# The first loads on two queues and x transposed one piece ahead, in fixed order: one encoder layer in exact-split fp32, one Trainium2 core

## The chip, the cores and the metric

The kernel runs on one core of a Trainium2 chip. The metric is the device time of one execution in microseconds (us). The engines of the core are named as the profile names them: PE is TensorE (PEld its weight loads), DVE is VectorE, ACT is ScalarE, POOL is GpSimd, SP is SyncE, whose queue issues DMAs.

## The reference

One layer on 256 tokens with 2048 channels: a gated bidirectional recurrence (HGRN2) as mixer, then a gated MLP with a depthwise convolution, each between RMS norms and with a residual.

```python
h = rmsnorm(x, norm_pre_mix)                   # (256, 2048)
u = h @ w_in                                   # (2048, 10240): q | f_fwd | f_bwd | i | g
m = gated(bidirectional_recurrence(u)) @ w_out
x = x + rmsnorm(m, norm_post_mix)
h = rmsnorm(x, norm_pre_ffn)
up = dwconv3(h @ ffn_w_in, ffn_w_conv)         # (2048, 11264)
x = x + rmsnorm((silu(gate) * val) @ ffn_w_out, norm_post_ffn)
```

This document is about the beginning alone: the first two products, which are columns of `q` and of `f_fwd`.

## The kernel before, in words

**Weights.** Every matrix is cut into chunks of 512 columns, and a chunk into *parts* of 256 rows (two k-blocks of 128). `load` fetches four k-blocks, one megabyte, into a tile `raw` (three buffers), which makes two parts. `prep` splits a part into a high and a low half: ScalarE rounds it to `whi` (L129, CAST), VectorE subtracts to give `wlo` (L130). There are four buffers of each. The first `raw` is loaded in four pieces of 256 KB and the second in two of 512 KB; from the third on a load is one DMA of a megabyte. So the first `raw` holds parts 0 and 1, the second parts 2 and 3, the third (the first whole megabyte) parts 4 and 5.

**x.** `xs` holds x as it is in memory, tokens on partitions, loaded in pieces of 256, 256, 512, 512 and 512 columns by `load_x`. `split_x(k2)` turns one *piece* of 256 columns: four PE transposes into a PSUM tile `tp` (L287), two ScalarE instructions that scale it into the high half of `xx` (L291), and two of VectorE that make the low half (L295). The scale comes from `prm`, a table of parameters. Part s of a product needs piece s of `xx`.

**The product.** `gemm_t` runs over eight parts; in each, for four column blocks n and two k-blocks, one matmul with `whi` (L204, 512 columns wide) and one with `wlo` (L206, 256 wide), sixteen a part. The first product takes a `pre` that is called at the head of part s and turns a piece ahead. Each later product looks three parts ahead with `prep`, the first one none (`LOOK if ci else 1`).

**Order.** A scheduler puts the instructions of each engine into an order at build time, by priorities that follow the program's order and by its own estimate of times; on the chip each engine then runs its list in that order. `tc.keep_in_program_order` fixes the place of an instruction against the others so marked. Semaphores are set by the framework: a DMA that uses one of eight DMA semaphores again first waits for the DMA that had it before.

The matmuls of `warm` (L266) run while the first data are on their way.

Of the kernel before, what the change touches and what calls it, by code (L numbers as in the profile page):

```python
# [18 lines left out]
P = 128  # L19
T = 256  # L20
D = 2048
KT = D // P
# [19 lines left out]
C_CW = C_LB + 2 * NH  # L42
# [4 lines left out]
def encoder_layer(  # L47
# [12 lines left out]
    nc = tc.nc  # L60
# [17 lines left out]
    prm = const.tile([P, C_END], F32, name="prm")  # L78
    ident = const.tile([P, P], F32, name="ident")
# [22 lines left out]
    def step():  # L102
        if soon or later:
            (soon or later).popleft()()

    def load(pieces=1):
        ci, s = subs[at["load"]]
        wd, c, _ = chunks[ci]
        raw = wraw.tile([P, 4, 512], F32, name="raw", tag="raw")
        src = wd[c, s // 2].rearrange("p (k n) -> p k n", n=512)  # L110
        w = 4 // pieces
        raws[ci, s // 2] = raw
        at["load"] += 2
        for i in range(pieces):
            nc.sync.dma_start(raw[:, w * i : w * i + w], src[:, w * i : w * i + w])
            yield

    def prep(upto):
        while at["prep"] < min(upto, len(subs)):
            i = at["prep"]  # L120
            if at["load"] <= i:
                list(load())
            ci, s = subs[i]
            src = raws[ci, s // 2][:, 2 * (s % 2) : 2 * (s % 2) + 2, :]
            pl, sfx = (extra[0], str(s)) if ci == C_UP - 1 and s >= 2 * chunks[ci][2] - 4 else (wspl, "")
            hi = pl.tile([P, 2, 512], F32R, name="whi", tag="whi" + sfx)
            lo = pl.tile([P, 2, 512], F32R, name="wlo", tag="wlo" + sfx)
            for j in [slice(0, 1), slice(1, 2)] if i == 0 else [slice(0, 2)]:
                S.copy(hi[:, j], src[:, j])  # L129
                V.tensor_tensor(lo[:, j], src[:, j], hi[:, j].bitcast(F32), op=ALU.subtract)  # L130
            parts[ci, s] = (hi, lo)
            at["prep"] += 1
# [3 lines left out]
    def flush():  # L136
        while soon or later:
            step()
# [46 lines left out]
    def gemm_t(xx, need=None, pre=None):  # L185


        ci = at["chunk"]
        at["chunk"] += 1
        nsub = 2 * chunks[ci][2]  # L190
        base = subs.index((ci, 0))
        ps = [ps_g.tile([P, 2, T], F32, name="pg", tag="pg") for _ in range(4)]
        for s in range(nsub):
            if s == need:
                flush()
            if pre:
                pre(s)
            prep(base + s + (LOOK if ci else 1))
            hi, lo = parts[ci, s]
            for n in range(4):  # L200
                cs = slice(n * P, (n + 1) * P)
                for j in range(2):
                    k = 2 * s + j
                    nc.tensor.matmul(ps[n], hi[:, j, cs], xx[:, k], start=(k == 0), stop=False)  # L204
                    last = k == 2 * nsub - 1
                    nc.tensor.matmul(ps[n][:, 0, :], lo[:, j, cs], xx[:, k, 0, :], start=False, stop=last)  # L206
            step()
        return ps
# [29 lines left out]
    xx = acts.tile([P, KT, 2, T], F32R, name="xx", tag="xx")  # L238
# [3 lines left out]
    xs = spool.tile([P, 2, D], F32, name="xs")  # L242

    def load_x(a, b):
        nc.sync.dma_start(xs[:, :, a:b], x_v[:, :, a:b])

    nc.sync.dma_start(prm[:, :C_CW], par[:, :C_CW])
    load_x(0, 256)
    first = load(4)
    next(first), next(first)  # L250
    load_x(256, 512)
    list(first)
    load_x(512, 1024)
    list(load(2))
    load_x(1024, 1536)
    load_x(1536, 2048)
# [25 lines left out]
    def split_x(k2):  # L282
        tp = ps_t.tile([P, 2, T], F32, name="tp", tag="tp")
        for j in range(2):
            k = 2 * k2 + j
            for m in range(2):
                nc.tensor.transpose(tp[:, j, m * P : (m + 1) * P], xs[:, m, k * P : (k + 1) * P], ident)  # L287
        for j in range(2):
            k = 2 * k2 + j
            w1 = prm[:, C_PRE + k : C_PRE + k + 1]  # L290
            S.activation(xx[:, k, 0, :], tp[:, j, :], AF.Copy, scale=w1)  # L291
        for j in range(2):
            k = 2 * k2 + j
            w1 = prm[:, C_PRE + k : C_PRE + k + 1]
            V.scalar_tensor_tensor(  # L295
                xx[:, k, 1, :], tp[:, j, :], w1, xx[:, k, 0, :].bitcast(F32), op0=ALU.mult, op1=ALU.subtract
            )
# [3 lines left out]
    def square_x(q):  # L301
        for m in range(2):
            jk = spool.tile([P, 512], F32, name="jk", tag="jk", bufs=2)
            i = 4 * m + q
            c = slice(q * 512, (q + 1) * 512)
            tc.keep_in_program_order(S.activation(jk, xs[:, m, c], AF.Square, accum_out=ss1[:, i : i + 1]))

    def mean_x():
# [3 lines left out]
        soon.extend([nop, lambda: spread(rs1, r1)])  # L312

    split_x(0)
    split_x(1)
    ps0 = gemm_t(xx, pre=lambda s: split_x(s + 2) if 2 * s + 4 < KT else None)
    soon.extend([lambda q=q: square_x(q) for q in range(4)] + [mean_x])
    ps1 = gemm_t(xx)
    load_rest()
    sstack.close()  # L320
# [26 lines left out]
    def do_q(g):  # L347
        ps = gemm_t(xx) if g else ps0
        qT = hp.tile([P, HG, T], F32, name="qT", tag="qT")
        each_token(ps, qT, r1)  # L350
        sg = nat.tile([P, HG, T], F32, name="qn", tag="qn")
        S.activation(sg, qT, AF.Sigmoid)
        V.tensor_tensor(qT, qT, sg, op=ALU.mult)
        st["q", g] = qT
# [174 lines left out]
    ps0 = gemm(oo, need=6)  # L529
# [84 lines left out]
    ps0 = gemm(hh, "head")  # L614
# [58 lines left out]
    ps0 = gemm(gg, need=20)  # L673
# [74 lines left out]
```

## Time and profile before

| | us |
|---|---|
| median of 3 runs | 1379.18 (1378.73 to 1380.75) |
| the profiled execution | 1379.42 |
| its span, first to last instruction | 1377.6 |
| TensorE busy in it | 1364.7 |
| end of the first product, q | 35.5 |
| end of the second product, f | 58.5 |

Span and rows are of one profiled execution. A row of the timeline has start and duration in us, engine, line, operation, output and inputs, and in brackets the idle time ahead of it with what ended it. A row of waits has who waited for whom, the total, the number of times and the longest. A row of DMA issues has the count, the size of one and the time from issue to landing. A row of stretches has busy time and count of PE, PEld, DVE, ACT and POOL, then TensorE's granted clock, the share of the DMA engines and GB/s.

### The profile page before, as it was taken

The page shows a single profiled execution, that of the slowest core. Times are in us where ns is not written, and L with a number is a line of the kernel's source. Part 1 is how long each engine was busy: PE and PEld are TensorE (multiplying, and loading weights), DVE is VectorE, ACT ScalarE, POOL GpSimd, SP SyncE. Part 2 cuts the span into 40 slices and gives each one's busy share as a digit, 9 for nine tenths or more (in the row PEclk, how much of TensorE's full clock was granted, in tenths as well). Part 3 has the DMA queues.
Part 4 walks back from the last instruction along what each step waited for, and adds up shares of the span by engine and source line. Part 5 has one row for each costly group of instructions (what it writes and reads, how often), then busy time and mean ns, then how long its engine had stood idle before and what let it go on. Part 6 is the DMA issues. An engine that isn't in the chain of part 4 may idle for free.

```text
span 1377.6 us, 18400 instructions
## 1 busy us (share of the span) xinstructions
PE 1364.7 (99%) x7362; PEld 1176.7 (85%) x7362; DVE 934.6 (68%) x1188; ACT 694.6 (50%) x971; POOL 13.5 (1%) x21
## 2 busy tenths in 40 slices
PE   8999999999999999999999999999999999999997
PEld 7888988898898888888888888888888888888886
DVE  6587668866886876567768676777677775445444
ACT  5644455454554544456656455555555554434442
POOL 0000000000000000000000000000000000000000
PEclk9999999999999999999999999999999999999999
DMA  7554355435534444673555545555555556555552
GB/s 286 180 187 149 125 181 184 153 123 183 184 134 168 166 144 153 245 245 109 197 183 184 193 176 210 183 186 182 188 186 192 194 190 214 191 204 185 189 207 93
DMA packets 36998, 248.93 MB, mean 181 GB/s; under 512 B 4144, under 2 KB 4912, under 8 KB 7472
## 3 DMA queue, kind: packets, MB, share of 16 engines
q1 hardware_dynamic: 36912, 247.75, 51.0%
q8 instruction: 58, 0.95, 0.3%
q14 instruction: 28, 0.23, 0.0%
HBM read 245.63 MB, written 2.10 MB: 180 GB/s over the span
## 4 chain that ended last, share of the span: by engine, by line
PE 97%; DVE 1%; issue 1%; ACT 0%; DMA 0%; SPq 0%; DVEq 0%; POOLq 0%; POOL 0%
PE pg L204 35%; PE pg L206 18%; PE pg L178 13%; PE pg L177 13%; PE pg L174 13%; PE sc L432 4%; PE sc L489 1%; PE sc L457 1%; PE sc L488 1%; PE sc L412 1%; DMA raw<-in_w_in 0%; PE tp L230 0%; PE tp L584 0%; PE tp L287 0%; DVE fw L685 0%
## 5 line engine op out<-in xcount | busy, mean ns | idle before, releaser
L130 DVE TENSOR_TENSOR wlo<-raw,whi 128x1024 fp32r<-128x1024 f32 (+1 forms) x457 | 555.2, 1221 | 381.6 <-ACT whi L129 374.8
L129 ACT CAST whi<-raw 128x1024 fp32r<-128x1024 f32 (+1 forms) x457 | 478.6, 1049 | 499.9 <-PE pg L204 259.3
L204 PE MATMUL pg<-hh,whi 128*128 128x512 f32 x1344 | 467.3, 397 | 0.0
L206 PE MATMUL pg<-hh,wlo 128*128 128x256 f32 x1344 | 366.1, 280 | 0.0
L204 PEld LDWEIGHTS pg<-hh,whi 128*128 128x128 f32 x1344 | 249.5, 188 | 56.2
L204 PE MATMUL pg<-xx,whi 128*128 128x512 f32 x768 | 270.0, 398 | 0.0
L206 PEld LDWEIGHTS pg<-hh,wlo 128*128 128x128 f32 x1344 | 253.4, 189 | 4.7
L206 PE MATMUL pg<-xx,wlo 128*128 128x256 f32 x768 | 211.0, 283 | 0.6 <-DVE wlo L130 0.6
L204 PEld LDWEIGHTS pg<-xx,whi 128*128 128x128 f32 x768 | 143.4, 188 | 30.7 <-DVE xx L295 0.4
L206 PEld LDWEIGHTS pg<-xx,wlo 128*128 128x128 f32 x768 | 145.4, 189 | 3.5 <-DVE wlo L130 1.1
L174 PE MATMUL pg<-whi,gg 128*128 128x512 f32 x352 | 137.0, 389 | 0.0
L178 PE MATMUL pg<-whi,gg 128*128 128x512 f32 x352 | 136.9, 389 | 0.0
L177 PE MATMUL pg<-wlo,gg 128*128 128x512 f32 x352 | 136.9, 389 | 0.0
L177 PE MATMUL pg<-wlo,xx 128*128 128x512 f32 x256 | 101.0, 394 | 0.0
L174 PE MATMUL pg<-whi,xx 128*128 128x512 f32 x256 | 100.2, 391 | 0.0
L178 PE MATMUL pg<-whi,xx 128*128 128x512 f32 x256 | 100.0, 391 | 0.0
L174 PEld LDWEIGHTS pg<-whi,gg 128*128 128x128 f32 x352 | 66.1, 188 | 13.9
L177 PEld LDWEIGHTS pg<-wlo,gg 128*128 128x128 f32 x352 | 66.1, 188 | 13.7
L178 PEld LDWEIGHTS pg<-whi,gg 128*128 128x128 f32 x352 | 66.1, 188 | 13.7
L432 PEld LDWEIGHTS sc<-qs,kc 128*128 128x128 f32 x448 | 57.7, 192 | 1.7
L432 PE MATMUL sc<-qs,kc 128*128 128x128 f32 x448 | 58.5, 285 | 0.0
L639 ACT ACTIVATE acc<-un,prm 128x256 f32<-128x256 f32 x84 | 38.2, 503 | 38.9 <-DVE un L345 38.8
(128 smaller groups left out, 1174.9 us busy)
## 6 DMA issues: line engine op xcount, KB each, us to landing
raw<-in_w_up SPq DMA_DIRECT2D x88, 1024.0 KB, 4.9
raw<-in_w_in SPq DMA_DIRECT2D x78, 1024.0 KB, 4.9
raw<-in_w_dn SPq DMA_DIRECT2D x44, 1024.0 KB, 4.9
raw<-in_w_o SPq DMA_DIRECT2D x16, 1024.0 KB, 4.9
x<-in_x SPq DMA_DIRECT2D x1, 2048.0 KB, 7.9
wp<-in_post SPq DMA_DIRECT2D x2, 1024.0 KB, 5.7
out<-fw SPq DMA_DIRECT2D x8, 256.0 KB, 2.6
xs<-in_x SPq DMA_DIRECT2D x3, 512.0 KB, 8.8
```

The lines of the kernel that those rows point to most:

```text
L129: S.copy(hi[:, j], src[:, j])
L130: V.tensor_tensor(lo[:, j], src[:, j], hi[:, j].bitcast(F32), op=ALU.subtract)
L174: mm = nc.tensor.matmul(ps[m], a, hi[:, j, :], start=(k == 0), stop=False)
L177: nc.tensor.matmul(ps[m], a, lo[:, j, :], start=False, stop=False)
L178: nc.tensor.matmul(ps[m], b, hi[:, j, :], start=False, stop=(k == 2 * nsub - 1))
L204: nc.tensor.matmul(ps[n], hi[:, j, cs], xx[:, k], start=(k == 0), stop=False)
L206: nc.tensor.matmul(ps[n][:, 0, :], lo[:, j, cs], xx[:, k, 0, :], start=False, stop=last)
L412: nc.tensor.matmul(sc[:, j, :], kc[0][:, h, sl], q[:, h, sl], start=True, stop=True)
L432: nc.tensor.matmul(sc[:, j, :], kc[0][:, h, sl], r, start=True, stop=True)
L457: nc.tensor.matmul(sc[:, h, :], ks[:, d, h, s0 : s0 + P], qs[:, 1 - d, h, t0 : t0 + P], start=True, stop=True)
L488: nc.tensor.matmul(o[:, h, :], Sd[:, 2 * h + b, :], v[:, b, cs], start=True, stop=False)
L639: S.activation(a, z, AF.Copy, scale=cw[1])
```

## The change

Two things. The four DMAs of the first `raw`, and the small one of `prm` between them, are issued from ScalarE's queue, and the pieces of x go first on SyncE's. And `split_x` is called for the piece of the next part alone, between the second and third of the four column blocks of a part (before: two pieces ahead of the loop, and piece s+2 at the head of part s); the transposes, and of each pair of k-blocks the first matmul with `whi`, are kept in program order. All lines behind move by two or three: L287, L291, L295 become L290, L295, L299, and L206 becomes L208.

```diff
-    def load(pieces=1):
+    def load(pieces=1, queue=nc.sync):
...
         for i in range(pieces):
-            nc.sync.dma_start(raw[:, w * i : w * i + w], src[:, w * i : w * i + w])
+            queue.dma_start(raw[:, w * i : w * i + w], src[:, w * i : w * i + w])
             yield
...
         for s in range(nsub):
             if s == need:
                 flush()
-            if pre:
-                pre(s)
             prep(base + s + (LOOK if ci else 1))
             hi, lo = parts[ci, s]
             for n in range(4):
+                if pre and n == 2:
+                    pre(s)
                 cs = slice(n * P, (n + 1) * P)
                 for j in range(2):
                     k = 2 * s + j
-                    nc.tensor.matmul(ps[n], hi[:, j, cs], xx[:, k], start=(k == 0), stop=False)
+                    mm = nc.tensor.matmul(ps[n], hi[:, j, cs], xx[:, k], start=(k == 0), stop=False)
+                    if pre and j == 0:
+                        tc.keep_in_program_order(mm)
...
-    nc.sync.dma_start(prm[:, :C_CW], par[:, :C_CW])
     load_x(0, 256)
-    first = load(4)
+    first = load(4, nc.scalar)
     next(first), next(first)
+    nc.scalar.dma_start(prm[:, :C_CW], par[:, :C_CW])
     load_x(256, 512)
     list(first)
...
             for m in range(2):
-                nc.tensor.transpose(tp[:, j, m * P : (m + 1) * P], xs[:, m, k * P : (k + 1) * P], ident)
+                tc.keep_in_program_order(
+                    nc.tensor.transpose(tp[:, j, m * P : (m + 1) * P], xs[:, m, k * P : (k + 1) * P], ident)
+                )
...
     split_x(0)
-    split_x(1)
-    ps0 = gemm_t(xx, pre=lambda s: split_x(s + 2) if 2 * s + 4 < KT else None)
+    ps0 = gemm_t(xx, pre=lambda s: split_x(s + 1) if 2 * s + 2 < KT else None)
```

What the scheduler makes of it is shown in rows of the built programs, with the semaphores that an instruction waits for. The numbers at names count tiles.

SyncE's queue at the start, before (`raw_87` is the first `raw`, `raw_94` the second, `raw_287` the first whole megabyte):

```order
L247 DMA prm_76<-in_par 128x65
L245 DMA xs_84<-in_x 128x2x256
L115 DMA raw_87<-in_w_in 128x512 x2
L245 DMA xs_84<-in_x 128x2x256
L115 DMA raw_87<-in_w_in 128x512 x2
L245 DMA xs_84<-in_x 128x2x512
L115 DMA raw_94<-in_w_in 128x1024 [waits DMAHW0_49]
L115 DMA raw_94<-in_w_in 128x1024 [waits DMAHW1_49]
L245 DMA xs_84<-in_x 128x2x512 [waits DMAHW2_49]
L245 DMA xs_84<-in_x 128x2x512 [waits DMAHW3_49]
L115 DMA raw_287<-in_w_in 128x2048 [waits DMAHW4_49]
```

Now, SyncE's queue (`raw_94` is still the second, `raw_269` the first whole megabyte):

```order
L247 DMA xs_84<-in_x 128x2x256 x2
L247 DMA xs_84<-in_x 128x2x512
L115 DMA raw_94<-in_w_in 128x1024
L115 DMA raw_94<-in_w_in 128x1024 [waits DMAHW0_49]
L247 DMA xs_84<-in_x 128x2x512 [waits DMAHW2_49]
L247 DMA xs_84<-in_x 128x2x512 [waits DMAHW3_49]
L115 DMA raw_269<-in_w_in 128x2048 [waits DMAHW4_49]
```

Five issues have left it. They stand at the head of ScalarE's list now, ahead of its table load and the first casts; the last of them waits for the first piece of x (DMAHW1):

```order
L115 DMA raw_86<-in_w_in 128x512 x2
L252 DMA prm_76<-in_par 128x65
L115 DMA raw_86<-in_w_in 128x512
L115 DMA raw_86<-in_w_in 128x512 [waits DMAHW1_49]
L129 ACT_TABLE_LOAD
L129 CAST whi_151<-raw_86 128x512 [waits DMAHW0_49]
L129 CAST whi_151<-raw_86 128x512 [waits DMAHW3_49]
```

ScalarE further on, before: the casts for parts 1 to 4 (`whi_200`, `229`, `258`, `289`) and the scalings of pieces 1 to 4 (`tp_147`, `160`, `191`, `220`):

```order
L291 ACTIVATE xx_80<-tp_147,prm_76 128x256 [waits PE_49]
L291 ACTIVATE xx_80<-tp_147,prm_76 128x256
L129 CAST whi_200<-raw_87 128x1024 [waits DMAHW6_49,DMAHW5_49]
L129 CAST whi_229<-raw_94 128x1024 [waits DMAHW0_49]
L291 ACTIVATE xx_80<-tp_160,prm_76 128x256 [waits PE_49]
L291 ACTIVATE xx_80<-tp_160,prm_76 128x256
L129 CAST whi_258<-raw_94 128x1024 [waits DMAHW1_49]
L291 ACTIVATE xx_80<-tp_191,prm_76 128x256 [waits PE_49]
L291 ACTIVATE xx_80<-tp_191,prm_76 128x256
L291 ACTIVATE xx_80<-tp_220,prm_76 128x256 [waits PE_49]
L291 ACTIVATE xx_80<-tp_220,prm_76 128x256
L129 CAST whi_289<-raw_287 128x1024 [waits DMAHW4_49,DVE_49]
```

Now: the casts for parts 1 to 5 are `whi_182`, `211`, `240`, `271`, `300`, the scalings of pieces 1 and 2 `tp_165` and `tp_194`:

```order
L129 CAST whi_182<-raw_86 128x1024 [waits DMAHW7_49,DMAHW1_49]
L129 CAST whi_211<-raw_94 128x1024 [waits DMAHW6_49]
L129 CAST whi_240<-raw_94 128x1024 [waits DMAHW0_49]
L295 ACTIVATE xx_80<-tp_165,prm_76 128x256 [waits PE_49]
L295 ACTIVATE xx_80<-tp_165,prm_76 128x256
L129 CAST whi_271<-raw_269 128x1024 [waits DMAHW4_49,PE_49,Activation_49]
L295 ACTIVATE xx_80<-tp_194,prm_76 128x256 [waits PE_49]
L295 ACTIVATE xx_80<-tp_194,prm_76 128x256
L129 CAST whi_300<-raw_269 128x1024 [waits DVE_49,PE_49]
```

The scaling of piece 1 has moved behind the casts for parts 1 to 3, that of piece 2 behind the cast for part 4; VectorE's list has its subtractions and low halves in the same new order.

TensorE at the seam of parts 0 and 1, now: the transposes of piece 1 in the middle of part 0, and behind its other half the first matmul of part 1, which waits for VectorE.

```order
L290 MATMUL tp<-ident,xs 128x128 [waits DMAHW2_49,PE_49]
L290 MATMUL tp<-ident,xs 128x128 x3
L204 MATMUL pg<-xx,whi 128x512
L208 MATMUL pg<-xx,wlo 128x256
L204 MATMUL pg<-xx,whi 128x512
L208 MATMUL pg<-xx,wlo 128x256
L204 MATMUL pg<-xx,whi 128x512
L208 MATMUL pg<-xx,wlo 128x256
L204 MATMUL pg<-xx,whi 128x512
L208 MATMUL pg<-xx,wlo 128x256
L204 MATMUL pg<-xx,whi 128x512 [waits DVE_49]
```

Before, two pieces were turned ahead of part 0 (eight transposes in a row) and the others stood one or two parts ahead of their own. From the second product on the lists of all engines are as before but for small exchanges (the load of the masks and one of weights, two squares of x and one cast).

## The prediction

> **What bounds the kernel now.** I read the page's busy times first, then TensorE's waits at the start, the timeline of TensorE over the first 60 us, the stretches with clock and DMA share, and last ScalarE's, VectorE's and SyncE's rows there.
>
> ```profile
> span 1377.6 us, 18400 instructions
> PE 1364.7 (99%) x7362; PEld 1176.7 (85%) x7362; DVE 934.6 (68%) x1188; ACT 694.6 (50%) x971; POOL 13.5 (1%) x21
> ```
> ```profile
> PE tp L287 <- DMA xs<-in_x: 2.8, 1, 2.8
> PE tp L266 <- POOL ident masks.py:199: 1.4, 1, 1.4
> PE pg L206 <- DVE wlo L130: 0.6, 1, 0.6
> ```
> TensorE is idle for 12.9 us of the span, and these are all its waits in the first 100 us. What a change at the start gains or loses is therefore what it does to the time at which TensorE has done its first two products, q and f. Each has eight parts (L204 and L206, sixteen matmuls a part).
>
> ```profile
> 4.99 0.60 PE L287 MATMUL tp<-ident,xs 128*128 128x128 f32 x4
> 8.38 1.08 PE L287 MATMUL tp<-ident,xs 128*128 128x128 f32 x4 [2.78 <-DMA xs<-in_x]
> 9.51 0.79 PE L204 MATMUL pg<-xx,whi 128*128 128x512 f32 x1
> ...
> 16.98 0.39 PE L204 MATMUL pg<-xx,whi 128*128 128x512 f32 x1
> ...
> 18.36 0.60 PE L287 MATMUL tp<-ident,xs 128*128 128x128 f32 x4
> 18.72 0.47 PE L204 MATMUL pg<-xx,whi 128*128 128x512 f32 x1
> ...
> 20.19 0.39 PE L204 MATMUL pg<-xx,whi 128*128 128x512 f32 x1
> ...
> 35.52 0.40 PE L204 MATMUL pg<-xx,whi 128*128 128x512 f32 x1
> ...
> 58.52 0.39 PE L204 MATMUL pg<-xx,whi 128*128 128x512 f32 x1
> ```
> Counting matmuls, part 0 starts at 9.51, part 2 at 16.98, part 3 at 20.19; the product q ends at 35.52 and f at 58.52. A part without transposes lasts (58.52 - 35.52)/8 = 2.87; a part with four transposes in its middle lasts 20.19 - 16.98 = 3.21, of which 1.83 lie from the first transpose (18.36) to the next part.
>
> ```profile
> 4.71:8.12 3.41, 0.88 (x8) 0.64 (x6) 0.69 (x1) 1.16 (x3) 0.00 (x0) 1.00 0.93 280
> 8.12:11.54 3.42, 3.12 (x10) 2.46 (x11) 2.68 (x6) 2.59 (x6) 0.00 (x0) 0.50 0.97 356
> 11.54:14.95 3.41, 3.41 (x23) 2.98 (x22) 2.22 (x2) 1.14 (x2) 0.00 (x0) 1.00 1.07 419
> 1.00:2.00 1.00, 0.64 (x3) 0.64 (x4) 0.00 (x0) 1.00 (x1) 0.29 (x1) 1.00 0.14 25
> 2.30:4.00 1.70, 1.70 (x10) 1.70 (x9) 1.07 (x5) 0.23 (x1) 0.00 (x0) 1.00 0.84 287
> 4.00:6.00 2.00, 1.59 (x11) 1.35 (x9) 0.51 (x4) 0.62 (x1) 0.00 (x0) 1.00 0.71 194
> 14.00:15.00 1.00, 1.00 (x10) 0.91 (x9) 0.76 (x1) 0.13 (x1) 0.00 (x0) 1.00 1.14 444
> 14.00:19.00 5.00, 5.00 (x35) 4.55 (x34) 3.65 (x6) 2.52 (x5) 0.00 (x0) 1.00 1.04 417
> ```
> The last three columns are clock, DMA share and GB/s. After a stretch with TensorE idle for 2.78 us the clock is 0.50 for 3.41 us. The DMA engines are full (share about 1) from 6 us on, and only partly used before.
>
> **The loads.** The same bytes are loaded as before.
>
> ```profile
> 0.74 0.39 SPq L247 DMA_DIRECT2D prm<-in_par  x1
> 1.18 0.42 SPq L245 DMA_DIRECT2D xs<-in_x  x1
> 8.26 0.34 SPq L115 DMA_DIRECT2D raw<-in_w_in  x1
> raw<-in_w_in SPq DMA_DIRECT2D x1, 1024.0 KB, 10.7
> xs<-in_x SPq DMA_DIRECT2D x1, 256.0 KB, 2.6
> 0.73 1.28 ACT L275 ACT_TABLE_LOAD   x1 [0.73 <-PEq L738]
> ```
> The load issued at 8.26 is the first whole megabyte of weights, for parts 4 and 5; it lands at 8.26 + 10.7 = 18.9. Ahead of it in both kernels stand all of x and two megabytes of weights, with it 5.28 MB. Five issues leave SyncE's queue for ScalarE's, so the first piece of x is issued at 0.74 in place of 1.18: 0.44 earlier. How long an issue takes on ScalarE no row shows; SyncE's take 0.39 to 0.47, so five take 0 to 2.3. I take 0.45 each; it hides, because the fifth waits anyway for the first piece of x. Two queues at once may also fill the engines' unused share, 1.70 x 0.16 + 2.00 x 0.29 = 0.85 us. So that megabyte lands between 18.9 - 0.44 = 18.5 and 17.6; I take the middle, 18.1. The far lower end is 5.28 MB at 417 GB/s from 1.7 on (an estimate of the first bytes at a start of 0.74, by the 25 GB/s of the second us), 14.4; the far upper end is no head start, 18.9.
>
> The Trainium skill (DMA: Bandwidth & Descriptors, "Issuing engines are not separate DMA queues") says that all issuers share the same 16 engines, and that issuing from several saves only the sequencer's issue time. By that rule the landing is 18.5 and the sum below 0.4 larger; the share of 1.04 from 14 to 19 agrees, while the 0.71 from 4 to 6 leaves room for more.
>
> **The first part.** ScalarE now issues four loads, waits for the first piece of x (1.18 + 2.6 = 3.8 before; now 0.74 + 2.6 and the same bytes of weights beside it, 0.26 MB at 194 to 444 GB/s, so 4.0 to 4.6), issues the fifth, then loads its table (1.28), casts two half pieces, and scales x. That gives 0.45 + 1.28 + 0.62 + 0.62 + 0.84, and 0.04 + 0.44 + 0.10 through VectorE to TensorE, 4.4 after the landing: part 0 starts at 8.4 to 9.0, 0.5 to 1.1 earlier than 9.51. It gains nothing: even with the clock at 0.50 throughout a window (1.7 lost) part 0 and its transposes end by 9.0 + 3.2 + 1.7 = 13.9, and what follows starts later.
>
> **The stall.** Program order decides here.
>
> ```profile
> 12.45 1.05 ACT L129 CAST whi<-raw 128x1024 fp32r<-128x1024 f32 x1 [1.18 <-DMA raw<-in_w_in]
> 14.87 0.84 ACT L291 ACTIVATE xx<-tp,prm 128x256 fp32r<-128x256 f32 x2 [1.36 <-PE tp L287]
> 19.00 0.84 ACT L291 ACTIVATE xx<-tp,prm 128x256 fp32r<-128x256 f32 x2 [1.62 <-PE tp L287]
> 16.68 1.23 DVE L130 TENSOR_TENSOR wlo<-raw,whi 128x1024 fp32r<-128x1024 f32 x1
> 19.88 0.88 DVE L295 SCALAR_TENSOR_TENSOR xx<-tp,prm,xx 128x256 fp32r<-128x256 f32 x2 [1.19 <-ACT xx L291]
> 5.25 0.62 ACT L129 CAST whi<-raw 128x512 fp32r<-128x512 f32 x1 [2.05 <-DMA raw<-in_w_in]
> ```
> At 12.45 a cast holds ScalarE for its weights' landing, with all behind it. Before, the scalings of x pieces 3 and 4 stand ahead of the cast for part 4. Now the scaling of piece 1 stands behind the casts of parts 1, 2 and 3, and that of piece 2 behind the cast of part 4; on VectorE likewise. So part 1 waits for the weights of part 3, and part 2 for the megabyte that only part 4 needs.
>
> Part 2: landing 18.1, cast 1.05, VectorE's subtraction 1.23 (ScalarE's scaling of 0.84 lies beside it), scaling on VectorE 0.44 for the first half, three hand-overs of 0.03 and one of 0.10: 2.9, so 21.0 in place of 16.98. Part 1 is earlier by two half megabytes of x and the megabyte, 2.1 MB at 417 GB/s = 5.0; it starts at 16.0, lasts 3.21 and ends at 19.2, so TensorE stands idle 2 to 4 us ahead of part 1 and 1.8 ahead of part 2.
>
> Then parts 2 to 4. From the first transpose to the next part TensorE has 1.83 of work; piece s+1 needs 0.64 (18.36 to 19.00) + 0.84 + 0.04 + 0.44 + 0.10 = 2.06. So each part waits 0.23 where nothing fills it: ahead of parts 3, 4, 5, together 0.7. Ahead of parts 6 and 7 half a part of f stands in between. That wait has no row before; its ends are 0 and, with a cast still running, 1.05 each; the chain above is nearest.
>
> From part 2 to the end of f: 3 x (3.21 + 0.23) + 2 x 3.21 + 2.87 + 23.0 = 42.6. So f ends at 21.0 + 42.6 = 63.6 in place of 58.52, **5.1 us later**. After that the order on every engine is as before but for one load of masks that changes place with one of weights; weights there arrive well ahead, I cost it at nothing, and if they came late the price is a wait like the 0.6 in the table of waits. TensorE is full for the rest, so the 5.1 stays. The profiled execution took 1379.42, 1.8 more than its span and 0.24 more than the median; 1379.42 + 5.1 = 1384.5, against the median 1384.3, which I forecast (likeliest case alone 1382.8 to 1385.4).
>
> **Rivals.** In short, the sum is (landing of that megabyte) - 13.0.
> - *The clock falls again.* The idle 1.8 to 2 us may leave TensorE at 0.50 in part 2; a window of 3.41 at half clock costs up to 1.7. In part 1 it is hidden by the wait for the megabyte. For it: 2.78 idle in one window sufficed. Against: 1.8 leaves the window half busy, and the next row with a busy 3.12 of 3.42 let it rise. Time 1384.3 + 1.7 = 1386.0. 22 in 100. The Trainium skill (TensorE: Matmul & The Clock Gate, "HAM oscillation") warns only of idle gaps above about 3.4 us; by that there is no fall, but the trace's gap of 2.78 differs, so I keep the chance.
> - *Two queues hurry the data, and the change is not slower.* If 5.28 MB land by 13.0 the loss is nil, and by 15.8 it is under 0.2%. At 444 GB/s, the best single us, from 1.7 on they land at 13.6: 1379.2 + 0.6 = 1379.8. Against: from 6 us on the engines' share is full already, and the slower rate up to then would have to double. 12 in 100.
> - *ScalarE isn't held at all* (casts find their weights there): then the start's 0.5 to 1.1, the 0.6 wait and the 1.0 or so lost at half clock could be saved, less 0.7 at the parts' seams: about 1377.5. The cast row with its 1.18 wait speaks against it. 3 in 100.
>
> **How the numbers follow.** The stall as summed 63, with the clock's fall 22, data hurried 12, not held 3. 0.2% is 2.8 us, about what a measurement of this kernel can tell from no change. Slower by more: 63 + 22, less a few where data come by 15.8, plus a few of the third: 0.85. Same 0.12, faster 0.03. The range reaches from a landing at 15.5 (1379.2 + 2.5 = 1381.7) to the clock's case with a landing at 18.9 (1379.2 + 5.9 + 1.7 = 1386.8).
>
> **What would show it.** In the changed profile: ScalarE's cast with a wait of about 2 us or more for the third megabyte, the scaling row behind it; TensorE waiting for VectorE's scaling 2 to 4 us ahead of part 1 and 2 ahead of part 2, then 0.2 each; part 2 near 21, the end of f near 63.6; first matmul of part 0 under 9.1. Wrong, if that megabyte lands under 16, if TensorE's waits sum to under 2 us after part 0, or if a new wait stands beyond 65 us.

## The result and the profile after

The changed kernel takes **1386.93 us** (median of 6 runs, 1385.88 to 1387.66) against 1379.5 for the kernel before on the same chip (6 runs, 1378.73 to 1380.75): ratio **1.0052, 95% interval 1.0041 to 1.0062**. It is slower, as forecast, and by more than forecast: 1386.93 lies 2.6 above the 1384.3 predicted and, in us, 0.1 above the upper end of the range. As a ratio it lies inside: 1.0052, where that end, 1386.8, is 1.0055 of 1379.18, since the kernel before took 0.3 more here than in its first runs. The profiled executions took 1386.11 and 1379.42, 6.7 apart.

The page's first lines of the changed kernel: the span has grown by 6.7 us, TensorE's busy time by 2.2.

```profile
span 1384.3 us, 18405 instructions
PE 1366.9 (99%) x7362; PEld 1177.4 (85%) x7362; DVE 934.3 (67%) x1188; ACT 694.8 (50%) x971; POOL 14.5 (1%) x21
```

TensorE's waits in its first 100 us (who waited for whom, us in total, times, longest), and with them one row of its weight loads, which is needed for the seams:

```profile
PE pg L204 <- DVE xx L299: 7.0, 2, 4.4
...
PEld pg L204 <- DVE xx L299: 9.2, 6, 4.8
...
```

Two waits for VectorE's scaling of x have taken the place of the one wait of 2.8 for x itself; the two other rows of TensorE's matmuls (1.4 and 0.6) are as before. Where they stand is told by TensorE's timeline (rows at which the wait or a part begins; counting matmuls, parts 0, 1, 2 and 3 start at 10.67, 18.10, 21.75 and 25.41, q ends at 42.19 and f at 65.13):

```profile
5.25 1.06 PE L290 MATMUL tp<-ident,xs 128*128 128x128 f32 x4
10.67 0.79 PE L204 MATMUL pg<-xx,whi 128*128 128x512 f32 x1 [4.36 <-DVE xx L299]
...
13.40 0.66 PE L290 MATMUL tp<-ident,xs 128*128 128x128 f32 x4
...
18.10 0.50 PE L204 MATMUL pg<-xx,whi 128*128 128x512 f32 x1 [2.65 <-DVE xx L299]
...
21.20 0.40 PE L204 MATMUL pg<-xx,whi 128*128 128x512 f32 x1
...
21.75 0.50 PE L204 MATMUL pg<-xx,whi 128*128 128x512 f32 x1
...
22.23 0.47 PE L204 MATMUL pg<-xx,whi 128*128 128x512 f32 x1
...
22.65 0.40 PE L204 MATMUL pg<-xx,whi 128*128 128x512 f32 x1
...
...
25.41 0.50 PE L204 MATMUL pg<-xx,whi 128*128 128x512 f32 x1
...
65.13 0.39 PE L204 MATMUL pg<-xx,whi 128*128 128x512 f32 x1
```

The end of f is 65.13 - 58.52 = 6.61 later, the span 6.7: nearly everything is lost in the first product, and 0.1 behind f. Part 0 is 1.2 later than before, part 1 4.8, part 2 4.8, part 3 5.2.

Why part 1 waits is read on the two engines ahead of it. ScalarE's timeline of the changed kernel, then VectorE's:

```profile
2.25 2.71 ACTq L115 DMA_DIRECT2D raw<-in_w_in  x2
4.98 1.28 ACT L129 ACT_TABLE_LOAD   x1 [4.98 <-DMA xs<-in_x]
...
9.27 0.84 ACT L295 ACTIVATE xx<-tp,prm 128x256 fp32r<-128x256 f32 x2 [0.93 <-DMA prm<-in_par]
...
13.08 2.94 ACT L129 CAST whi<-raw 128x1024 fp32r<-128x1024 f32 x3 [2.73 <-DMA raw<-in_w_in]
15.92 0.83 ACT L295 ACTIVATE xx<-tp,prm 128x256 fp32r<-128x256 f32 x2
18.57 1.05 ACT L129 CAST whi<-raw 128x1024 fp32r<-128x1024 f32 x1 [1.82 <-DMA raw<-in_w_in]
20.34 0.84 ACT L295 ACTIVATE xx<-tp,prm 128x256 fp32r<-128x256 f32 x2 [0.72 <-PE tp L290]
```
```profile
14.15 3.50 DVE L130 TENSOR_TENSOR wlo<-raw,whi 128x1024 fp32r<-128x1024 f32 x3 [1.99 <-ACT whi L129]
17.57 0.87 DVE L299 SCALAR_TENSOR_TENSOR xx<-tp,prm,xx 128x256 fp32r<-128x256 f32 x2
...
21.21 0.88 DVE L299 SCALAR_TENSOR_TENSOR xx<-tp,prm,xx 128x256 fp32r<-128x256 f32 x2 [0.33 <-ACT xx L295]
```

The transposes of piece 1 were done at 14.06. But ScalarE stood from 10.35 to 13.08 at the cast for part 1, whose weights had not landed, and then did the casts for parts 1, 2 and 3 in a row; VectorE did their three subtractions, 3.50 us, and only at 17.57 the low half that part 1 needs. Two of the three casts were for parts that TensorE reached at 21.75 and 25.41.

The DMA issues of the first 14 us (who, how many, size, median us from issue to landing), where `prm`, the table that every scaling needs, took 7.4 us in place of 1.8:

```profile
raw<-in_w_in SPq DMA_DIRECT2D x1, 1024.0 KB, 8.9
...
prm<-in_par ACTq DMA_DIRECT2D x1, 32.5 KB, 7.4
```

The whole megabyte was issued at 9.53 and landed at 18.47. Stretches of the changed kernel (busy PE, PEld, DVE, ACT, POOL, then clock, DMA share and GB/s):

```profile
2.00:4.00 2.00, 2.00 (x12) 2.00 (x11) 0.00 (x0) 0.00 (x0) 0.00 (x0) 1.00 0.89 265
4.00:6.00 2.00, 2.00 (x11) 1.91 (x9) 0.00 (x0) 1.02 (x1) 0.00 (x0) 1.00 0.93 197
6.70:10.10 3.40, 0.00 (x0) 0.00 (x0) 1.58 (x4) 1.65 (x4) 0.00 (x0) 1.00 1.04 395
10.12:13.53 3.41, 2.86 (x9) 2.47 (x10) 1.89 (x7) 0.68 (x2) 0.00 (x0) 0.50 1.03 399
13.53:16.94 3.41, 1.92 (x13) 1.47 (x11) 2.79 (x3) 3.22 (x5) 0.00 (x0) 1.00 1.07 411
```

### The profile page after: what moved, and what is told of

Read it like the earlier page. It is cut to its first block, busy times and chain, and to the rows that moved or that the text cites. A ratio compares the mean times of both kernels' runs of the same rounds, so it can differ in the third digit from the quotient of the medians.

```text
span 1384.3 us, 18405 instructions
## 1 busy us (share of the span) xinstructions
PE 1366.9 (99%) x7362; PEld 1177.4 (85%) x7362; DVE 934.3 (67%) x1188; ACT 694.8 (50%) x971; POOL 14.5 (1%) x21
## 4 chain that ended last, share of the span: by engine, by line
PE 97%; DMA 1%; DVE 1%; issue 1%; ACT 0%; DVEq 0%; POOLq 0%; POOL 0%
PE pg L204 35%; PE pg L208 18%; PE pg L177 12%; PE pg L174 12%; PE pg L178 12%; PE sc L435 4%; DMA raw<-in_w_in 1%; PE sc L492 1%; PE sc L460 1%; PE sc L491 1%; PE sc L415 1%; PE tp L232 0%; DMA xs<-in_x 0%; PE tp L587 0%; DVE wlo L130 0%
## 5 line engine op out<-in xcount | busy, mean ns | idle before, releaser
L208 PE MATMUL pg<-hh,wlo 128*128 128x256 f32 x1344 | 366.1, 280 | 0.0
L208 PEld LDWEIGHTS pg<-hh,wlo 128*128 128x128 f32 x1344 | 253.4, 189 | 4.7
L208 PE MATMUL pg<-xx,wlo 128*128 128x256 f32 x768 | 211.1, 283 | 0.6 <-DVE wlo L130 0.6
L208 PEld LDWEIGHTS pg<-xx,wlo 128*128 128x128 f32 x768 | 145.6, 190 | 3.6 <-DVE wlo L130 1.1
```

## The experiments

Each was compared with the kernel before on one chip. Executions of one and the same kernel differ by 1 to 3 us, so beside the medians stands the end of f in the profiled execution, which shows where a difference arises. It is one execution of each kernel. For the changed kernel and those with the order alone, the casts one part ahead, two pieces on ScalarE and the turn a quarter earlier, that execution took 0.8 to 1.5 less than the median, so their ends of f understate what the medians lose; why their other executions are longer stays open.

| kernel | median us | before beside it | ratio (95%) | end of f | against before |
|---|---|---|---|---|---|
| before | | | | 58.52 | |
| the change | 1386.93 | 1379.5 | 1.0052 (1.0041 to 1.0062) | 65.13 | +6.61 |
| queues alone | 1381.49 | 1379.42 | 1.0014 (1.0004 to 1.0023) | 60.44 | +1.92 |
| order alone | 1382.54 | 1379.42 | 1.0018 (1.0009 to 1.0028) | 60.62 | +2.10 |
| casts one part ahead | 1384.64 | 1379.42 | 1.0035 (1.0022 to 1.0048) | 62.71 | +4.19 |
| two pieces on ScalarE | 1383.34 | 1379.42 | 1.0029 (1.0018 to 1.0040) | 60.95 | +2.43 |
| table on SyncE | 1382.86 | 1380.08 | 1.0020 (1.0011 to 1.0029) | 61.85 | +3.33 |
| turned a quarter earlier | 1381.20 | 1380.08 | 1.0008 (0.9999 to 1.0017) | 59.16 | +0.64 |
| start in order of need | 1379.08 | 1380.08 | 0.9993 (0.9984 to 1.0002) | 58.67 | +0.15 |
| piece ahead of cast | 1378.63 | 1379.68 | 0.9995 (0.9986 to 1.0004) | 57.66 | -0.86 |

### The two halves of the change apart

*Queues alone*: the kernel before with the first `raw` and `prm` on ScalarE's queue, x turned as before.

```diff
-    nc.sync.dma_start(prm[:, :C_CW], par[:, :C_CW])
     load_x(0, 256)
-    first = load(4)
+    first = load(4, nc.scalar)
     next(first), next(first)
+    nc.scalar.dma_start(prm[:, :C_CW], par[:, :C_CW])
```

> Only the loads move to ScalarE's queue; x is turned two pieces ahead as before. Theory A (the loss of 6.6 us at the end of f has three parts: the last quarter of the first weights lands 3.2 later on ScalarE's queue, two casts stand needlessly ahead of the scaling of piece 1, and each seam of parts waits 0.45): that quarter lands near 13 again, part 0 starts near 10.7 since the small table lands near 9.2, but no scaling stands behind the casts of parts 2 and 3 and there are no seams, so f ends near 59.5, +0.5 to +1.5 us on before. Theory B (two queues slow the loads as a whole, and that is most of the loss): +4 us or more.

*Order alone*: the changed kernel with all of these loads on SyncE's queue, as before.

```diff
+    nc.sync.dma_start(prm[:, :C_CW], par[:, :C_CW])
     load_x(0, 256)
-    first = load(4, nc.scalar)
+    first = load(4)
     next(first), next(first)
-    nc.scalar.dma_start(prm[:, :C_CW], par[:, :C_CW])
```

> Only the new order of the pieces of x; all loads on SyncE as before. Theory A: part 0 starts near 9.5, part 1 near 13.5, no wait for the casts of parts 2 and 3 (the scaling of piece 1 stands ahead of them in this build), seams of 3.65 in place of 3.21 for four or five parts: f ends near 60.6, +2 us on before. Theory B: no loss, 0. Rival C (the fixed order is the whole loss): +5 to +7 us.

The queues alone cost 1.92 at the end of f, the order alone 2.10. ScalarE's row and TensorE's of the kernel with the queues alone show how: part 0 starts at 10.57, since the table landed at 9.07.

```profile
9.16 1.57 ACT L291 ACTIVATE xx<-tp,prm 128x256 fp32r<-128x256 f32 x4 [1.08 <-DMA prm<-in_par]
...
15.12 2.94 ACT L129 CAST whi<-raw 128x1024 fp32r<-128x1024 f32 x3
```
```profile
10.57 0.80 PE L204 MATMUL pg<-xx,whi 128*128 128x512 f32 x1 [1.77 <-DVE xx L295]
...
12.66 0.63 PE L204 MATMUL pg<-xx,whi 128*128 128x512 f32 x1
```

Here x is turned early, so the scalings of three pieces stand ahead of the same three casts, and once part 0 has begun TensorE waits for nothing. That part starts 1.06 later, and a wide matmul takes 0.63, as at half clock (the one at 14.00 still 0.60), where before the slow stretch ended at 11.5: from the part's start some 1.6 us more at half pace, or 0.8 lost. The two make up nearly all of the 1.92, which is 0.4 above the most that was expected; the expectation had no term for the clock. In the kernel with the order alone, ScalarE's list alternates (its timeline), and a cast holds no scaling for long:

```profile
9.51 1.05 ACT L129 CAST whi<-raw 128x1024 fp32r<-128x1024 f32 x1 [1.29 <-DMA raw<-in_w_in]
11.98 0.84 ACT L295 ACTIVATE xx<-tp,prm 128x256 fp32r<-128x256 f32 x2 [1.43 <-PE tp L290]
13.13 1.05 ACT L129 CAST whi<-raw 128x1024 fp32r<-128x1024 f32 x1 [0.31 <-DMA raw<-in_w_in]
```

Its parts 0 to 3 start at 8.79, 13.80, 17.23 and 20.88: part 1 is not held, and most of what is lost is lost at the seams, that is, where one part ends and the next begins, of which below. So 1.92 + 2.10 = 4.0 of the 6.61 are the sum of the two halves, and 2.6 belong to neither. The medians say the same: 2.07 and 3.12 of 7.43, and 2.2 left. Of these three kernels only the one with both halves has three casts ahead of the scaling of piece 1.

### The casts held to one part ahead

The changed kernel, with the casts and subtractions of parts 1 and later fixed in turn with the scalings, none more than one part ahead. (`keep_in_program_order` fixes an instruction behind the one that the program gives its engine just before.)

```diff
-                S.copy(hi[:, j], src[:, j])
-                V.tensor_tensor(lo[:, j], src[:, j], hi[:, j].bitcast(F32), op=ALU.subtract)
+                c1 = S.copy(hi[:, j], src[:, j])
+                c2 = V.tensor_tensor(lo[:, j], src[:, j], hi[:, j].bitcast(F32), op=ALU.subtract)
+                if ci == 0 and s:
+                    tc.keep_in_program_order(c1)
+                    tc.keep_in_program_order(c2)
...
-            prep(base + s + (LOOK if ci else 1))
+            prep(base + s + (LOOK if ci else 2))
...
(and so for the two scalings in split_x where k2 is not 0)
```

> The changed kernel with the casts and subtractions of the first product at most one part ahead and pinned in turn with the scalings, so that the scaling of piece 1 stands behind the cast of part 1 alone. Theory A: part 1 starts near 16.0 in place of 18.1, part 2 near 19.6, f ends near 63.0: 2.1 us under the changed kernel, +4.5 to +5 on before. If the casts ahead were not what held the scaling: no gain on the changed kernel. Theory B: the same as the changed kernel.

The end of f came 2.42 earlier, at 62.71. ScalarE's timeline of this kernel: one cast, then the scaling, where three casts stood.

```profile
12.45 1.05 ACT L129 CAST whi<-raw 128x1024 fp32r<-128x1024 f32 x1 [2.92 <-DMA raw<-in_w_in]
13.67 0.84 ACT L298 ACTIVATE xx<-tp,prm 128x256 fp32r<-128x256 f32 x2 [0.17 <-PE tp L293]
14.40 1.04 ACT L129 CAST whi<-raw 128x1024 fp32r<-128x1024 f32 x1
```

Part 1 starts at 15.51 in place of 18.10, part 2 at 18.97 in place of 21.75, and TensorE no longer waits ahead of part 1: its last matmul of part 0 is at 15.39. So the two casts too early cost 2.4 to 2.8, about the share that the halves left open. Three things blur the size: the first `raw`'s last piece landed at 12.43 here and at 13.05 in the changed kernel, and `prm` at 8.35 in place of 9.18, each of which helps by up to 0.8; and the clock stood at 0.50 from 8.1 to 14.9 here, 3.4 longer, which hurts. Of the 2.09 by which f still ends later than with the order alone, 1.71 stand at the start of part 1 already (15.51 against 13.80): a later part 0 and its half clock, not a wait for a scaling.

### Why the weights and the table are late

The last quarter of the first `raw` landed at 9.82 before and at 13.05 after. *Two pieces on ScalarE*: the changed kernel, with the last two of its four pieces back on SyncE's queue.

```diff
-            queue.dma_start(raw[:, w * i : w * i + w], src[:, w * i : w * i + w])
+            (queue if i < 2 else nc.sync).dma_start(raw[:, w * i : w * i + w], src[:, w * i : w * i + w])
```

> The changed kernel, but only the first two quarters of the first weights (and the small table) are issued by ScalarE; the last two go on SyncE's queue behind the first half of x. TensorE's order is the same, instruction for instruction. Theory A: the last quarter lands near 9.5, the scaling of piece 1 is free of the casts of parts 2 and 3, part 1 starts at 12.4 to 13.3, the seams stay at 3.65: f ends at 59.4 to 60.4, +1 to +2 us on before and about 5 under the changed kernel. Theory B: half the bytes that ScalarE's queue had are left on it, so half the loss, +3. Rival C (the order on TensorE with its seams is the loss): as the changed kernel, +6.

*Table on SyncE*: the changed kernel, with `prm` alone back at the head of SyncE's queue.

```diff
+    nc.sync.dma_start(prm[:, :C_CW], par[:, :C_CW])
     load_x(0, 256)
     first = load(4, nc.scalar)
     next(first), next(first)
-    nc.scalar.dma_start(prm[:, :C_CW], par[:, :C_CW])
```

> The changed kernel with the small table of parameters back at the head of SyncE's queue; the four quarters of the first weights stay on ScalarE's. With the table early the scheduler also puts the scaling of piece 1 ahead of the casts of parts 2 and 3. Theory A (late last quarter, plus casts in the way, plus seams): part 0 starts near 8.8 in place of 10.7 and gains nothing by it; the last quarter still lands near 12.5 to 13, so part 1 starts near 15.8 and f ends near 63.0, 2.1 us under the changed kernel and 4.5 on before. Rival (the late start of part 0, by the late table, is what the loads on two queues cost): f ends at 61 or less.

ScalarE's timeline of the first of them, and of the second:

```profile
2.16 1.28 ACT L129 ACT_TABLE_LOAD   x1 [2.16 <-issue]
...
7.67 0.84 ACT L295 ACTIVATE xx<-tp,prm 128x256 fp32r<-128x256 f32 x2 [0.81 <-DMA prm<-in_par]
9.04 1.05 ACT L129 CAST whi<-raw 128x1024 fp32r<-128x1024 f32 x1 [0.53 <-DMA raw<-in_w_in]
```
```profile
2.67 1.28 ACT L277 ACT_TABLE_LOAD   x1 [2.67 <-issue]
...
8.23 0.84 ACT L295 ACTIVATE xx<-tp,prm 128x256 fp32r<-128x256 f32 x2 [0.74 <-PE tp L290]
10.24 1.04 ACT L129 CAST whi<-raw 128x1024 fp32r<-128x1024 f32 x1 [1.17 <-DMA raw<-in_w_in]
```

In the changed kernel the issue of the last quarter waited on ScalarE's queue from 2.7 to 4.6 for the first piece of x (the row at 2.25 above, 2.71 long), and then landed 8.4 us later, among all that SyncE had issued in the meantime. Issued at 2.16 from ScalarE without that wait it lands at 10.16, issued at 2.26 from SyncE at 8.96; ScalarE's table load comes 2.3 to 2.8 earlier too. With that the cast for part 1 stands at 10.24 or 9.04 in place of 13.08. In both kernels the scheduler also put the scaling of piece 1 ahead of the casts for parts 2 and 3 (at 12.10 and 13.36, with two casts in a row behind it at 12.82 and 14.09). What the late weights cost by themselves is therefore not separated from what the order of the casts costs. The first kernel ends f at 60.95, above the 59.4 to 60.4 expected: its parts 1 to 3 start at 14.12, 17.55 and 21.21, 0.3 behind those of the order alone and with the same seams. Its median is 3.92 above before, twice the most expected and nearer the +3 of the rival; the trace, where the last quarter lands at 8.96, speaks against that rival, and the 1.5 between the profiled execution and the median are not explained. The second ends f at 61.85, between the 63.0 expected and the 61 of the rival, because taking one issue away also frees the last quarter of its wait. `prm` at the head of the queue landed at 4.0, but the first piece of x, behind it now, at 7.04 in place of 4.60, and TensorE's table of waits in this kernel has a new row for it:

```profile
PE tp L290 <- DMA xs<-in_x: 1.6, 1, 1.6
```

### The seams

The order alone with the piece turned one column block earlier, after a quarter of the part instead of half.

```diff
-                if pre and n == 2:
+                if pre and n == 1:
                     pre(s)
```

> The order alone (loads as before), with each piece turned after the first column block of the part ahead of its own in place of the second. Theory A (a seam waits because half a part, 1.47 us, is less than the way from transpose to scaled piece): a quarter part more, 0.70 us, covers it, the parts from 2 on fall from 3.65 to 3.2 us, f ends near 58.8 in place of 60.6: 0 to +0.5 us on before, 1.8 under the order alone. Rival (the pinned order itself slows TensorE at each part, by weight loads that can't go ahead): the parts stay at 3.65 and f ends near 60.6.

TensorE's timeline of this kernel, at the starts of parts 2 to 5: the distance is 3.25, 3.26 and 3.22, where the changed kernel has 3.66 (21.75 to 25.41). The seams are all but gone (a part with transposes took 3.21 before), and f ends 1.46 earlier than with the order alone, at 59.16, 0.4 above the 58.8 expected. Matmuls pinned in order run no slower for it, which was the rival.

```profile
17.23 0.39 PE L204 MATMUL pg<-xx,whi 128*128 128x512 f32 x1
...
20.48 0.40 PE L204 MATMUL pg<-xx,whi 128*128 128x512 f32 x1
...
23.74 0.40 PE L204 MATMUL pg<-xx,whi 128*128 128x512 f32 x1
...
26.96 0.39 PE L204 MATMUL pg<-xx,whi 128*128 128x512 f32 x1
```

### A start in the order of need

If the theory holds, a start that puts every instruction behind what is needed sooner should beat both kernels. This one has `prm` first and alone on ScalarE's queue and all else on SyncE's; part 0 does its first k-block for all columns before the second; piece s+1 is turned after the first quarter of part s (after half in part 0); the scaling of piece 0 is ahead of the second half cast; casts, scalings and matmuls are fixed in turn; and parts 1 and 2 do their eight matmuls with the high half before those with the low half.

```diff
+    nc.scalar.dma_start(prm[:, :C_CW], par[:, :C_CW])
     load_x(0, 256)
...
+            prep(base + s + (1 if s < 2 else 2))
...
+            if pre and s == 0:
+                todo = [(h, *q) for j in range(2) for q in nj([j]) for h in (1, 0)]
+            elif pre and s < 3:
+                todo = [(h, *q) for h in (1, 0) for q in nj([0, 1])]
+            else:
+                todo = [(h, *q) for q in nj([0, 1]) for h in (1, 0)]
+            for i, (h, n, j) in enumerate(todo):
...
+                if pre and i == (8 if s == 0 else 4):
+                    pre(s)
+                    if s:
+                        prep(base + s + (2 if s == 1 else 3))
```

> A version after the theory: large loads all on SyncE, the small table on ScalarE; part 0 runs its first k-block for all columns while the second quarter of the weights lands, the scaling of piece 0 is pinned ahead of the cast of that quarter, pieces are turned after the first quarter of a part, no scaling stands behind a cast for a later part than its own plus one, and parts 1 and 2 run all their high halves first. Theory A: part 0 starts near 7.1, part 1 near 11, part 2 near 14.5, f ends at 56.5 to 57.5: 1 to 2 us under before. Rival (the first loads bound the start, whatever the order): part 2 not under 16.5, f near 58.5, no gain.

It missed: f ended at 58.67, as late as before. Parts 0 to 2 started at 7.76, 11.75 and 15.24, 0.7 behind the expected but well ahead of before. ScalarE's timeline, then TensorE's, show one wait left:

```profile
20.32 1.05 ACT L129 CAST whi<-raw 128x1024 fp32r<-128x1024 f32 x1 [2.56 <-DMA raw<-in_w_in]
21.28 0.83 ACT L322 ACTIVATE xx<-tp,prm 128x256 fp32r<-128x256 f32 x2
```
```profile
23.08 0.50 PE L230 MATMUL pg<-xx,whi 128*128 128x512 f32 x1 [1.09 <-DVE xx L328]
```

I had made the same fault by hand: the scaling of piece 4 stood behind the cast of the whole megabyte, which landed at 20.24, and part 4 waited. The last run moves that cast behind the scaling, and lets parts 3 and 4 take their high halves first as well.

```diff
-                prep(base + s + (1 if s < 2 else 2))
+                prep(base + s + (2 if s == 2 or s > 3 else 1))
...
-            elif pre and s < 3:
+            elif pre and s < 5:
...
-                    if s:
+                    if s and s != 2:
```

> The kernel of the run before (start in the order of need) with one thing moved: in parts 1 and 3 the casts that come last in the part stand behind the scaling of the piece turned there, so that the scaling of piece 4 stands ahead of the cast of the first whole megabyte; parts 3 and 4 also do their eight matmuls with the high half first. Theory (the loss there was the 1.09 us that part 4 waited for a scaling held behind the cast of a late megabyte): that wait goes, part 4 starts near 21.9 in place of 23.08, the end of f comes at 57.5 to 57.8 in place of 58.67, and the time is 1.0 us less than that kernel's, 1.3 to 2.0 less than before's (ratio 0.9985 to 0.999). Rival (part 4 is limited by the megabyte itself, which lands at 20.2): the wait is then for the cast, part 4 starts at 22.6 or later, and the end of f at 58.2 or later.

ScalarE's timeline and TensorE's of it:

```profile
20.30 0.84 ACT L322 ACTIVATE xx<-tp,prm 128x256 fp32r<-128x256 f32 x2 [2.46 <-PE tp L317]
21.03 1.99 ACT L129 CAST whi<-raw 128x1024 fp32r<-128x1024 f32 x2
```
```profile
22.14 1.19 PE L230 MATMUL pg<-xx,whi 128*128 128x512 f32 x4
...
57.66 0.40 PE L230 MATMUL pg<-xx,whi 128*128 128x512 f32 x1
```

The wait is gone, part 4 starts at 22.14, and f ends at 57.66, 1.01 earlier than without this edit and 0.86 earlier than before; its span is 1376.8 against 1377.6. How much of the 1.01 is the moved cast and how much the high halves of parts 3 and 4 was not separated. Against the changed kernel, 1378.63 to 1386.93, all of the loss is back. The end of f came as expected, the time did not: 1.3 to 2.0 less than before were expected and the medians show 1.05, about as much as without this edit (1.00). Against the kernel before, 0.9995 (0.9986 to 1.0004) doesn't tell it from no change: the profile shows a gain of 0.9 us, and the timing cannot confirm one of that size.

## Why the prediction was right, and where it was not

**The mechanism was right in kind, and named the wrong landing.** A scaling that part 1 needs stood behind casts for later parts, in the order of ScalarE's list and again of VectorE's, and behind a cast that waited for its weights. Holding the casts back took 2.42 away; in another kernel a scaling behind a cast that waited for a megabyte held part 4 for 1.09, and that wait went with the edit that undid it. Which weights hold part 1, and whether the megabyte holds part 2, the prediction had wrong (below, under the hold).

**The loads.** The whole megabyte was predicted to land at 18.1, the middle of 18.5 and 17.6, and landed at 18.47. It gained 0.45, though it was itself issued 1.27 later (9.53 against 8.26). The rule of the Trainium skill (DMA: Bandwidth & Descriptors, "Issuing engines are not separate DMA queues"), that several issuers save only issue time, gave 18.5; here the trace agrees, and the middle that I took was a concession to the idle share that the rows did not repay. Before, the row from 2 to 4 us is

```profile
2.00:4.00 2.00, 2.00 (x12) 2.00 (x11) 1.07 (x5) 0.25 (x2) 0.00 (x0) 1.00 0.75 250
```

So the share rose there from 0.75 to 0.89 and the rate from 250 to 265 GB/s, and from 4 to 6 us the share from 0.71 to 0.93 and the rate only from 194 to 197. That 18.47 meets 18.5 so closely is in part luck: in the four other kernels with the first loads on two queues the same megabyte landed between 18.24 and 18.91, and not in the order in which their first piece of x was issued. None gained more than 0.7, and the rival of hurried data, which needed a landing by 15.8, falls with that.

**The first part.** Predicted at 8.4 to 9.0, measured at 10.67. The step that failed listed ScalarE's work behind the first piece of x and left out `prm`: moved behind two loads of 256 KB, it landed at 9.18 (before 2.50), and the scaling at 9.27 waited 0.93 for it. Another 0.82 is the wait of the second half cast, at 7.72, for its weights, to which the sum gave no landing either. That this part's time is hidden was right in the changed kernel, where part 1 waits for something else; with the queues alone it is where nearly all of the 1.92 arise.

**The hold.** Predicted idle: 2 to 4 ahead of part 1 and 1.8 ahead of part 2. Measured: 2.65 ahead of part 1 and no wait at the start of part 2. Two steps failed.
- Part 1 was put at 16.0, by the landing of part 3's weights (in size rightly, 13.28 against the 13.1 implied) and 2.9 behind it, the chain of one cast and one subtraction. But the landing that held ScalarE was another: the last quarter of the first `raw`, for part 1, at 13.05, before which none of the three casts could be done. From 13.28 to part 1 it took 18.10 - 13.28 = 4.8. The prediction gave that quarter no landing of its own. So three subtractions, 3.50, and not one of 1.23 stood ahead of the scaling on VectorE.
- Part 2 was put at 21.0, by the megabyte. The cast for part 4 did wait 1.82 for it, at 18.57, but by then part 1 had begun so late that it covered this: 18.10 + 3.65 = 21.75. The piece's transposes at 19.70 came after that cast. The sum "landing minus 13.0" thus named the wrong landing. That part 2 nevertheless came within 0.75 of the forecast 21.0 is luck: another landing and a longer chain led to nearly the same time.

**The seams.** Predicted 0.23 at three of them, behind part 2; measured 0.44 to 0.46 in each of the parts 1 to 4, and 0.23 in part 5. The first matmul of part 2 comes 0.55 after the matmul ahead of it where the step is 0.35, 0.20, which is about the 0.23 summed. What was left out is the other half: VectorE's row at 21.21 holds two instructions, the second ends at 22.09, and the matmul of the second k-block starts only after it (22.23 - 21.75 = 0.48, and 0.42 to the next). The rows of TensorE's matmul waits do not show this, since each wait is short. The row of its weight loads above shows the first half (six waits, the two holds and four of 0.35 to 0.38 at the seams); the second half is read from the distances between starts. From part 2 to the end of f that makes 43.38 in place of 42.6.

**The sum.** 21.75 + 43.38 = 65.13, against 21.0 + 42.6 = 63.6: the terms are short by 0.75 and 0.78. The rest beyond the end of f was costed at nothing and came to 0.1.

**The clock.** The rival in which it falls again in part 2 did not come in the profiled execution. It was at 0.50 from 10.1 to 13.5, as before in part 0 alone, and there the hold covers it. The stretches fit this: from 6.7 to 10.1 TensorE did nothing, and the next window was at 0.50. The wait of 2.65 ahead of part 1 left 1.92 of 3.41 busy and 2.25 of the next 3.41, and behind it a wide matmul takes 0.40, as at full clock. So in the profiled execution, 1386.11 against the 1384.5 forecast for it, the 1.6 too much are the 0.75, the 0.78 and the 0.1 above, and not the clock, though 1386.0 was that rival's time. For the median this is not shown: it lies 0.8 higher than the profiled execution, and the five other executions have a mean granted clock of 0.995 where that one has 0.997. A second fall in them is possible; they left no trace.

**What stays open.** Why executions of one kernel differ by 1 to 3 us is not known. That the scheduler put three casts ahead is seen in the built order, and what it costs was measured; by which of its estimates it did so was not tried. The cost of the late last quarter alone was not measured either.

## What to carry to other kernels

A list that an engine runs in order couples two streams: before moving a step later, look at what the scheduler will then put ahead of it, and whether that waits for a DMA; fix the order on every engine that the chain passes, not on TensorE alone, where this change fixed it. Price a step that is handed on through two halves by the second half too, and write down for each instruction that is moved every input it needs, the small tables as well. A small transfer that everything needs belongs at the head of a queue, here of the one that x does not use, and a DMA whose issue must wait does not belong on a queue whose engine has to compute.

## What was not expected of the hardware

- How long a small DMA takes depends on what was issued before and beside it, on any queue: the same 32.5 KB took 1.8 us at the head of SyncE's queue, 2.6 at the head of ScalarE's beside x (the last two kernels), 3.3 at the head of SyncE's with four weight loads beside it on ScalarE's, and 5.9 to 7.4 on ScalarE's behind two of these.
- The bytes moved in the first microseconds depended little on whether one queue issued or two: 250 and 265 GB/s from 2 to 4 us, 194 and 197 from 4 to 6, where the DMA engines were busy for 0.71 and for 0.93 of the time.
- The clock column can miss a fall: with the queues alone it reads 1.00 from 10.6 to 14.0, where wide matmuls take 0.63, the length that they have at 0.50 in the changed kernel (from 10.7 to 13.4); later they take 0.40.
- A wait of 2.78 was followed by a clock of 0.50 before, one of 2.65 was not after, and with the queues alone two of 1.40 and 1.77, 1.1 apart, were followed by matmuls of 0.63. What differs between the first two is how the wait lies in a stretch of 3.41: 0.88 of it busy before, 1.92 after. The Trainium skill (TensorE: Matmul & The Clock Gate, "HAM oscillation") warns of idle gaps above about 3.4 us; in the trace of before a shorter one, 2.78, was followed by the fall.
